# A decoder trunk on one core: the MLP's second product interleaved with the first of the next quarter, five of eight K-pairs by seven products, and PSUM banks given by number

## The chip, the core and the metric

One core of a Trainium2 chip. TensorE (PE) multiplies, VectorE (DVE) and ScalarE (ACT) prepare operands and evacuate results, SyncE (SP) issues the loads of the weights. The metric is device microseconds for the whole kernel; a run counts the slowest core, here the only one.

## The reference

A trunk of two layers over one residual stream, 256 tokens by 2048 features, all in float32. Each layer has a mixer and a squared-ReLU MLP, both behind an RMS norm:

```
x = x + mix(rms_norm(x, norm_mix[layer]))
x = x + squared_relu_mlp(rms_norm(x, norm_mlp[layer]), mlp_w1[layer], mlp_w2[layer])

def squared_relu_mlp(h, w1, w2):
    return jnp.square(jax.nn.relu(h @ w1)) @ w2      # 2048 -> 8192 -> 2048
```

The change touches the MLP alone, and the way PSUM banks are named in the whole kernel.

## The kernel before

Every operand is float32 and is split into a hi part (rounded to the matmul's format) and a lo part (the remainder). A product is then three matmuls: hi by hi, hi by lo, lo by hi (`mm_three`, L145). For weights, ScalarE makes hi (`wh`, L129) and VectorE subtracts to get lo (`wl`, L130). Tiles of weights come by DMA into four buffers (`raw`), and hi and lo have four buffers each.

The MLP (`mlp`, L996) goes through the 8192 hidden features in four quarters of 2048. A quarter has two stretches.

*First product.* Eight chunks of 256 hidden features. A chunk is four steps (`steps_feats`, L252), each with 16 matmuls of 512 columns (hi weights) and 16 of 256 columns (lo weights) for four K-tiles. Both feature blocks of a chunk accumulate in a PSUM bank of their own. `evac_h` then adds the two halves of the bank (`both`: `bt_h` on ScalarE, `hu` on VectorE), applies relu and square, and splits the result into hi and lo. For the first four pairs of K-tiles (`SEVEN = 4`) it builds eight combinations of the four 128x128 blocks of the pair (`hp`, `pt`); for the other pairs it keeps them as they are (`ht`).

*Second product.* Two halves, of two 512-column blocks of the output each (`steps_seven`, L188). In a half there are eight pairs of K-tiles. A pair with combinations is a *seven step* (L199): Strassen's scheme, seven block products of three matmuls, 21 matmuls of 512 columns. Its weights need sums first: `ta` (L214), `tb` (L216, L217), and hi and lo of them. The products go to four banks of `pmis` (`ym`) and to three of the four of `pacc` (`yc`). The other pairs are *ordinary*: two steps (`eight`) with 12 matmuls each, 24 in all. The order of steps is written in the code: seven, two ordinary, seven, two ordinary, seven, seven, and the rest. After the last seven step the four `ym` banks are combined and added to the residual (`early_y`), and after the last ordinary step the four `yc` banks (`late_y`).

In layer 1 the second half of the last quarter is the tail `finish`, without seven steps. In layer 0 the last half turns the new residual for the next layer (`nt_mix`) ahead of and behind its last step.

The program is a list of tiles and instructions; a scheduler puts each engine's instructions in an order of its own, and each engine then works its queue from front to end.

Of the kernel before, what the change touches and what calls it, by code (L numbers as in the profile page):

```python
# [9 lines left out]
F32 = mybir.dt.float32  # L10
# [4 lines left out]
P = 128  # L15
# [3 lines left out]
KD = D // P  # L19
FF = 8192  # L20
NQ = 4
SEVEN = 4
EPS = 1e-6
BIG = -3.0e38
MLA_SCALE = 192 ** -0.5
# [44 lines left out]
def trunk(ctx: ExitStack, tc: tile.TileContext, plan, a, c_first, c_even, c_odd, out):  # L70
# [3 lines left out]
    xpool = ctx.enter_context(tc.tile_pool(name="xpool", bufs=1))  # L74
    tpool = ctx.enter_context(tc.tile_pool(name="tpool", bufs=1))
    wpool = ctx.enter_context(tc.tile_pool(name="wpool", bufs=1))
    pacc = ctx.enter_context(tc.tile_pool(name="pacc", bufs=4, space=bass.MemoryType.PSUM))
    pmis = ctx.enter_context(tc.tile_pool(name="pmis", bufs=4, space=bass.MemoryType.PSUM))

    n_t = [0]  # L80
# [9 lines left out]
        n_t[0] += 1  # L90
        return mpool[0].tile([P, 2, S], FR, name=f"M{n_t[0]}", tag="M", bufs=17)

    def acc(name):
        return pacc.tile([P, 512], F32, name=name, tag="acc")

    def mis(name):
        return pmis.tile([P, 512], F32, name=name, tag="mis")
# [88 lines left out]

    def steps_seven(pool, H, pairs, w, c, early, late, name="y"):

        box = {}
        rest = [k for k in range(len(H) // 2) if k not in pairs]

        def seven(k):  # L200
            def go():
                first, last = k == pairs[0], k == pairs[-1]
                if first:
                    box["m"] = {i: mis(f"{name}m{i}") for i in (1, 5, 7, 6)}
                    box["c"] = {i: acc(f"{name}c{i}") for i in ((0, 1), (1, 0), (0, 0), (1, 1))}
                m, cc = box["m"], box["c"]
                pt = H[2 * k][0]
                r0 = load(w, [(2 * k, c, 512), (2 * k + 1, c + 512, 512)], (2, 512))
                r1 = load(w, [(2 * k, c + 512, 512), (2 * k + 1, c, 512)], (2, 512))
                n_w[0] += 1  # L210
                ta = pool.tile([P, 2, 512], F32, name=f"ta{n_w[0]}", tag="ta", bufs=2)
                tb = pool.tile([P, 2, 512], F32, name=f"tb{n_w[0]}", tag="tb", bufs=1)
                h0, l0 = halves(r0)
                nc.vector.tensor_tensor(ta, r0, r1[:, 0:1, :].to_broadcast([P, 2, 512]), OP.add)  # L214
                h1, l1 = halves(ta, pool, "t", 3)
                nc.vector.tensor_tensor(tb[:, 0, :], ta[:, 0, :], r0[:, 1, :], OP.add)  # L216
                nc.vector.tensor_tensor(tb[:, 1, :], tb[:, 0, :], r1[:, 1, :], OP.add)  # L217
                h2, l2 = halves(tb, pool, "t", 3)
                h3, l3 = halves(r1[:, 1:2, :])

                def product(ac, i, h, l, j, last):
                    mm_three(ac, (pt[:, 0, i, :], pt[:, 1, i, :]), (h[:, j, :], l[:, j, :]), first, last)

                end = last and not rest
                product(m[1], 1, h0, l0, 0, last)
                product(m[5], 5, h1, l1, 0, last)
                product(m[7], 4, h1, l1, 1, last)
                product(m[6], 6, h2, l2, 0, last)
                product(cc[1, 0], 3, h2, l2, 1, end)
                product(cc[0, 1], 7, h0, l0, 1, end)  # L230
                product(cc[0, 0], 0, h3, l3, 0, end)
                if last:
                    early(m[1], m[5], m[6], m[7])
            return go

        def eight(k, j):
            def go():
                cc = box["c"]
                hi, lo = weights(w, 2 * k, 2, c + 512 * j, 512)
# [8 lines left out]
        out, rest_of = [], iter(rest)  # L248
        for i, k in enumerate(pairs):
            out.append([seven(k)])  # L250
            if i != len(pairs) - 2:
                out += [[eight(r, j) for j in range(2)] for r in [next(rest_of)]]  # L252
        out += [[eight(r, j) for j in range(2)] for r in rest_of]
        return sum(out, [])

    def steps_feats(Ts, w, c0, evac, n=256, name="f"):

        box = {}
        groups = [range(i, i + 4) for i in range(0, len(Ts), 4)]

        def make(gi, g):
            def go():
                if gi == 0:
                    box["a"] = [acc(f"{name}{f}") for f in range(n // P)]
                hi, lo = weights(w, g[0], 4, c0, n)
# [157 lines left out]
    def weave(main, side):  # L423

        done = 0
        for i, go in enumerate(main):
            go()
            want = (i + 1) * len(side) // max(1, len(main))
            while done < want:
                side[done]()  # L430
                done += 1
        for go in side[done:]:
            go()

    class Late:
# [561 lines left out]
    def mlp(layer, norm, nxt):  # L997
# [6 lines left out]
        def evac_h(H):  # L1004
            def make(c):
                box = {}

                def go(f, ac):
                    u = sm.tile([P, S], F32, name="hu", tag="hu", bufs=2)
                    both(sm, u, ac, "h")  # L1010
                    nc.scalar.activation(u, u, AF.Relu)  # L1011
                    if c >= SEVEN:
                        r = sm.tile([P, S], F32, name="hr", tag="hr", bufs=2)
                        nc.scalar.activation(r, u, AF.Square)
                        H[2 * c + f] = sm.tile([P, 2, S], FR, name="ht", tag="ht", bufs=2 * (NF // 2 - SEVEN) + 1)
                        split_to(H[2 * c + f], r)
# [36 lines left out]

        def late_y(c):
            def go(cc):
                for b, j in ((1, 0), (0, 1), (0, 0), (1, 1)):
# [4 lines left out]
        def evac_y(c):  # L1061
# [2 lines left out]
                    nc.vector.scalar_tensor_tensor(x[b][c], ac[b], scale["s"][:, b:b + 1], x[b][c], OP.mult, OP.add)  # L1064
            return go

        for q in range(NQ):
            H = [None] * NF
            ev = evac_h(H)
            for c in range(NF // 2):  # L1070
                steps = steps_feats(X, ("mlp_w1", layer, 0), q * (FF // NQ) + c * 256, ev(c), name="h")
                if q == 0 and c == 0:
                    run(steps[:3])
                    norm.turn(3)
                    run(steps[3:])
                    norm.close()
                    scale["s"] = norm.inv_var()
                else:
                    run(steps)
            wq = ("mlp_w2", layer, q * (FF // NQ))  # L1080
            last = q == NQ - 1
            for c in (0, 2):
                if last and nxt is None and c == 2:
                    finish(H, wq, evac_y, scale, sm)
                    break
                steps = steps_seven(sm, H, list(range(SEVEN)), wq, c * 512, early_y(c), late_y(c))
                if last and c == 2:
                    nxt.stats(0)
                    nxt.stats(1)
                    steps = steps[:-1] + [lambda: nxt.turn(0)] + steps[-1:] + [lambda: nxt.turn(1)]  # L1090
                run(steps)
        if nxt is not None:
            nxt.stats(2)
            nxt.stats(3)
# [64 lines left out]
```

## Time and profile before

| | us |
|---|---|
| median of 3 runs | 2175.98 (2175.11 to 2176.67) |
| the profiled execution | 2174.26 |
| its span, first to last instruction | 2172.5 |
| TensorE busy | 2131.6 |
| VectorE busy | 1607.7 |
| ScalarE busy | 1216.2 |

Part 1 of the page gives the busy time of each engine as an average over the whole span; the stages differ, so the timeline and the windows have to be read stage by stage. Matmuls overlap in the records (one of 512 columns lasts about 0.39 us and the next starts about 0.23 us after it), so how fast TensorE goes is read from start to start. A row of the busy time by stage reads: stretch, its length, then busy us (instructions) of PE, PEld, DVE, ACT and POOL, the granted TensorE clock (1.00 is 2.4 GHz), the share of DMA and GB/s. In brackets behind a row of the timeline stands how long the engine was idle before it and what ended that.

### The profile page before, as it was taken

Reading aid. Unit: us, or ns where it says so; the run is one execution under the profiler, and the core shown is the slowest. Engines: PE = TensorE matmul, PEld = TensorE weight load, DVE = VectorE, ACT = ScalarE, POOL = GpSimd, SP = SyncE. Lnnn points to the kernel's source line nnn. Section 1 sums busy time; section 2 is a strip of 40 time slices with the busy share of each in tenths; the row PEclk is TensorE's granted clock in tenths of the full one; section 3 lists DMA queues with packets and bytes.
Section 4 is the critical chain, followed back from the end, with each engine's and each line's share of the span. In section 5 each row is a group of like instructions: output and inputs, shape, how many; then the busy total and the mean of one; then the engine's idle time right before and its main releaser. Section 6 shows DMA issues by size and latency. Waiting matters only on the chain.

```text
span 2172.5 us, 29631 instructions
## 1 busy us (share of the span) xinstructions
PE 2131.6 (98%) x11034; PEld 1826.3 (84%) x11034; DVE 1607.7 (74%) x2265; ACT 1216.2 (56%) x1833; POOL 5.6 (0%) x12
## 2 busy tenths in 40 slices
PE   9999999999999999999999999999999999999998
PEld 8988888887887887887888888888878878878887
DVE  5678556698679679768977667556896797698685
ACT  6676445654664565565644444556655655655664
POOL 0000000000000000000000000000000000000000
PEclk9999999999999999999999999999999999999999
DMA  8554455556555655655555555455555556556654
GB/s 293 168 175 162 158 180 184 186 173 208 190 184 186 202 179 180 207 182 181 187 193 174 176 173 175 165 185 184 184 192 196 184 176 212 185 178 208 206 186 153
DMA packets 115281, 404.53 MB, mean 186 GB/s; under 512 B 12929, under 2 KB 13569, under 8 KB 115137
## 3 DMA queue, kind: packets, MB, share of 16 engines
q1 hardware_dynamic: 114624, 401.07, 56.3%
q8 instruction: 87, 1.43, 0.3%
q0 software_dynamic: 368, 1.51, 0.2%
q14 instruction: 58, 0.47, 0.1%
q10 hardware_dynamic: 144, 0.06, 0.0%
HBM read 400.49 MB, written 2.10 MB: 185 GB/s over the span
## 4 chain that ended last, share of the span: by engine, by line
PE 78%; DVE 14%; DMA 4%; issue 3%; ACT 1%; SPq 0%; DVEq 0%; POOLq 0%; POOL 0%; ACTq 0%
PE h L158 19%; PE h L162 10%; DVE wl L130 7%; DMA wr<-in_mlp_w 4%; PE q L158 3%; PE k L158 3%; PE o L150 3%; PE o L148 3%; PE o L149 3%; PE v L148 2%; PE v L150 2%; PE v L149 2%; DVE ta L214 2%; PE k L162 1%; PE q L162 1%
## 5 line engine op out<-in xcount | busy, mean ns | idle before, releaser
L130 DVE TENSOR_TENSOR wl<-wr,wh 128x1024 fp32r<-128x1024 f32 (+4 forms) x769 | 884.2, 1155 | 429.1 <-ACT wh L129 422.2
L129 ACT ACTIVATE wh<-wr 128x1024 fp32r<-128x1024 f32 (+4 forms) x769 | 768.2, 1003 | 676.2 <-PE h L158 197.9
L158 PE MATMUL h<-T,wh 128*128 128x512 f32 x2048 | 513.4, 392 | 0.0
L158 PEld LDWEIGHTS h<-T,wh 128*128 128x128 f32 x2048 | 368.4, 189 | 66.9 <-DVE T L296 1.1
L162 PEld LDWEIGHTS h<-T,wl 128*128 128x128 f32 x2048 | 279.4, 190 | 20.0
L162 PE MATMUL h<-T,wl 128*128 128x256 f32 x2048 | 285.6, 282 | 0.0
L148 PE MATMUL ym<-wh,pt 128*128 128x512 f32 x240 | 95.2, 401 | 16.0 <-ACT wh L129 15.9
L149 PE MATMUL ym<-wl,pt 128*128 128x512 f32 x240 | 97.5, 406 | 10.8 <-DVE wl L130 10.7
L129 ACT ACTIVATE wh<-ta 128x1024 fp32r<-128x1024 f32 x60 | 63.6, 1061 | 77.3 <-DVE ta L214 77.2
L148 PE MATMUL o<-wh,M 128*128 128x512 f32 x256 | 102.3, 399 | 0.0
L214 DVE TENSOR_TENSOR ta<-wr,wr 128x1024 f32<-128x1024 f32 x60 | 73.3, 1221 | 37.1 <-DMA wr<-in_mlp_w 36.8
L129 ACT ACTIVATE wh<-tb 128x1024 fp32r<-128x1024 f32 x60 | 63.2, 1053 | 66.6 <-DVE tb L217 66.6
L150 PE MATMUL o<-wh,M 128*128 128x512 f32 x256 | 99.8, 390 | 0.0
L149 PE MATMUL o<-wl,M 128*128 128x512 f32 x256 | 99.7, 389 | 0.0
L150 PE MATMUL ym<-wh,pt 128*128 128x512 f32 x240 | 94.8, 395 | 0.0
L130 DVE TENSOR_TENSOR wl<-tb,wh 128x1024 fp32r<-128x1024 f32 x60 | 73.3, 1221 | 22.9 <-ACT wh L129 22.9
L1011 ACT ACTIVATE hu<-hu 128x256 f32<-128x256 f32 x128 | 50.5, 408 | 51.3 <-DVE hu L278 51.3
L148 PE MATMUL v<-wh,T 128*128 128x512 f32 x192 | 77.4, 403 | 0.0
L130 DVE TENSOR_TENSOR wl<-ta,wh 128x1024 fp32r<-128x1024 f32 x60 | 73.1, 1219 | 2.7 <-ACT wh L129 2.7
L150 PE MATMUL v<-wh,T 128*128 128x512 f32 x192 | 74.9, 390 | 0.0
L149 PE MATMUL v<-wl,T 128*128 128x512 f32 x192 | 74.8, 390 | 0.0
L148 PEld LDWEIGHTS ym<-wh,pt 128*128 128x128 f32 x240 | 44.9, 189 | 30.0 <-ACT wh L129 21.7
(991 smaller groups left out, 3644.2 us busy)
## 6 DMA issues: line engine op xcount, KB each, us to landing
wr<-in_mlp_w SPq DMA_DIRECT2D x512, 512.0 KB, 3.6
wr<-in_od_w_qkv SPq DMA_DIRECT2D x96, 512.0 KB, 4.1
wr<-in_ev_w_in SPq DMA_DIRECT2D x32, 512.0 KB, 3.5
wr<-in_ev_w_out SPq DMA_DIRECT2D x32, 512.0 KB, 3.4
wr<-in_od_w_out SPq DMA_DIRECT2D x32, 512.0 KB, 3.5
wr<-in_ev_w_in SPq DMA_DIRECT2D x24, 344.0 KB, 3.0
wr<-in_ev_w_in SPq DMA_DIRECT2D x15, 364.0 KB, 5.8
wr<-in_mla_w_ukv SPq DMA_DIRECT2D x8, 512.0 KB, 3.5
```

What stands on the lines that cost most here:

```text
L129: nc.scalar.activation(hi, raw, AF.Copy)
L130: nc.vector.tensor_tensor(lo, raw, hi.bitcast(F32), OP.subtract)
L148: nc.tensor.matmul(ac, xh, hi, start=first, stop=False)
L149: nc.tensor.matmul(ac, xh, lo, start=False, stop=False)
L150: nc.tensor.matmul(ac, xl, hi, start=False, stop=last)
L158: nc.tensor.matmul(acs[f], hi[:, j, f * P:(f + 1) * P], Ts[j].rearrange("p a t -> p (a t)"), start=first and j == 0, stop=False)
L162: nc.tensor.matmul(acs[f][:, :S], lo[:, j, f * P:(f + 1) * P], Ts[j][:, 0, :], start=False, stop=last and j == n - 1)
L214: nc.vector.tensor_tensor(ta, r0, r1[:, 0:1, :].to_broadcast([P, 2, 512]), OP.add)
L1011: nc.scalar.activation(u, u, AF.Relu)
```

## The change

Three things are changed, with the arithmetic of the reference kept.

1. `SEVEN` is 5: in a half five pairs are seven steps and three are ordinary. The last half of layer 0 has three and five.
2. A seven step is cut into two parts: `go_a` (loads, sums, splits, and products 1, 5 and 7 into `ym`; 9 matmuls) and `go_b` (products 6, 3, 2 and 4; 12 matmuls). The first product is cut into 16 blocks of 128 features, two steps of eight K-tiles each. `woven` runs blocks and parts of seven steps in turn: in the first half of a quarter the last eight blocks of that quarter, in the second half the first eight blocks of the next. The ordinary steps of a half follow together. The first half of the first quarter of a layer is still made in chunks of 256.
3. `acc` gives each of the four banks a tag of its own. Chunks elsewhere take the banks in turn; in the woven part products 3, 2 and 4 have banks 0, 1 and 2, and all blocks of the first product have bank 3, which goes to the fourth `yc` when the ordinary steps begin.

`hr` is no longer a tile of its own, the square is written in place; the late adds come in another order.

```diff
-SEVEN = 4
+SEVEN = 5
...
-    def acc(name):
-        return pacc.tile([P, 512], F32, name=name, tag="acc")
+    def acc(name, bank=None):
+
+        if bank is None:
+            bank = n_a[0] % 4
+            n_a[0] += 1
+        return pacc.tile([P, 512], F32, name=name, tag=f"acc{bank}", bufs=1)
...
+            def go_a():
                 if first:
                     box["m"] = {i: mis(f"{name}m{i}") for i in (1, 5, 7, 6)}
...
                 product(m[1], 1, h0, l0, 0, last)
                 product(m[5], 5, h1, l1, 0, last)
                 product(m[7], 4, h1, l1, 1, last)
+
+            def go_b():
+                if first:
+                    box["c"] = {i: acc(f"{name}c{i[0]}{i[1]}", n) for n, i in enumerate(((1, 0), (0, 1), (0, 0)))}
+                m, cc = box["m"], box["c"]
+                product(m[6], 6, *t[2], 0, last)
+                product(cc[1, 0], 3, *t[2], 1, end)
+                product(cc[0, 1], 7, *t[0], 1, end)
+                product(cc[0, 0], 0, *t[3], 0, end)
                 if last:
                     early(m[1], m[5], m[6], m[7])
...
+    def woven(main, side):
+
+        done = 0
+        for i, go in enumerate(main):
+            want = -(-(i + 1) * len(side) // len(main))
+            run(side[done:want])
+            done = want
             go()
...
+            def block(i):
+                def go():
+                    run(steps_feats(X, ("mlp_w1", layer, 0), q * (FF // NQ) + i * P,
+                                    lambda f, ac: ev[i // 2](i % 2, ac), n=P, name="h", kt=8, bank=3))
+                return go
...
         for q in range(NQ):
+            last = q == NQ - 1
+            wq = ("mlp_w2", layer, q * (FF // NQ))
+            seven, eight = steps_seven(sm, H, list(range(SEVEN)), wq, 0, early_y(0), late_y(0))
+            woven(hs[NF // 2:], sum(seven, []))
+            run(*eight)
+            if last and nxt is None:
+                finish(H, wq, evac_y, scale, sm)
+                break
+            pairs = list(range(3 if last else SEVEN))
+            seven, eight = steps_seven(sm, H, pairs, wq, 1024, early_y(2), late_y(2))
...
+            hs, _ = blocks(q + 1, H)
+            sv = sum(seven, [])
+            woven(hs[:NF // 2], sv)
+            run(*eight)
```

What this does to the queues is seen in the built programs' order. TensorE of before, layer 0, where the first product of the second quarter (`h`) ends and the second product begins (`ym` is a product of a seven step, `wl` and `wh` the halves of its weights):

```order
L162 MATMUL h_5919<-T_3623,wl_5989 128x256
L162 MATMUL h_5919<-T_3631,wl_5989 128x256
L162 MATMUL h_5919<-T_3634,wl_5989 128x256
L148 MATMUL ym_6028<-wh_6042,pt 128x512
L149 MATMUL ym_6028<-wl_6043,pt 128x512
L150 MATMUL ym_6028<-wh_6042,pt 128x512
L148 MATMUL ym_6029<-wh_6047,pt 128x512
```

TensorE of the change, layer 0, in the second half of the first quarter: the end of the third seven step's first products, and the fourth block `h` of the second quarter:

```order
L156 MATMUL ym_4806<-wh_5075,pt 128x512
L154 MATMUL ym_4807<-wh_5081,pt 128x512
L155 MATMUL ym_4807<-wl_5082,pt 128x512
L156 MATMUL ym_4807<-wh_5081,pt 128x512
L154 MATMUL yc_4842<-wh_5081,pt 128x512
L164 MATMUL h_5098<-T_3252,wh_5101 128x512
L164 MATMUL h_5098<-T_3255,wh_5101 128x512
```

One matmul of product 3 (`yc`) stands ahead of the block; its other two, and products 2 and 4, stand behind the block's 32 matmuls.

VectorE of before, layer 0, where the second half of the second quarter begins (`x` from `yc` is a late add; `ta` and `tb` are the sums of the first seven step; `wl` from `wr` is lo of plain weights):

```order
L130 TENSOR_TENSOR wl_6394<-wr_6387,wh_6393 128x1024
L1058 SCALAR_TENSOR_TENSOR x_73<-yc(0, 0)_6034,iv_mlp_3681,x_73 128x512
L1058 SCALAR_TENSOR_TENSOR x_77<-yc(1, 0)_6033,iv_mlp_3681,x_77 128x512
L214 TENSOR_TENSOR ta_6391<-wr_6387,wr_6389 128x1024
L130 TENSOR_TENSOR wl_6409<-wr_6389,wh_6408 128x512
L1058 SCALAR_TENSOR_TENSOR x_74<-yc(0, 1)_6032,iv_mlp_3681,x_74 128x512
L1058 SCALAR_TENSOR_TENSOR x_78<-yc(1, 1)_6035,iv_mlp_3681,x_78 128x512
L130 TENSOR_TENSOR wl_6399<-ta_6391,wh_6398 128x1024
L216 TENSOR_TENSOR tb_6392<-ta_6391,wr_6387 128x512
L130 TENSOR_TENSOR wl_6436<-wr_6433,wh_6435 128x1024
```

VectorE of the change, layer 0, second half of the first quarter: the queue between the evacuations (`hu`) of the second and the third block of the next quarter:

```order
L136 TENSOR_TENSOR wl_5076<-ta_5068,wh_5075 128x1024
L228 TENSOR_TENSOR tb_5069<-tb_5069,wr_5066 128x512
L136 TENSOR_TENSOR wl_5071<-wr_5064,wh_5070 128x1024
L1041 TENSOR_TENSOR hp<-hp 128x256
L136 TENSOR_TENSOR wl_5086<-wr_5066,wh_5085 128x512
L1042 TENSOR_TENSOR hp<-hp 128x128
L136 TENSOR_TENSOR wl_5082<-tb_5069,wh_5081 128x1024
L1043 TENSOR_TENSOR hp<-hp 128x128
L136 TENSOR_TENSOR wl_5102<-wr_5099,wh_5101 128x1024
L1046 TENSOR_TENSOR pt<-hp,pt 128x1024
L136 TENSOR_TENSOR wl_5124<-wr_5121,wh_5123 128x1024
L286 TENSOR_TENSOR hu<-h_5012,bt_h 128x256
```

Between two evacuations now stand the rest of the third seven step's weights, the combinations of a finished pair (`hp`, `pt`) and the weights of the next block (`wl_5102`, `wl_5124`); the last row frees bank 3.

## Rows read from the trace of the kernel before

**Rows 1.** The page, part 1: busy us (share) xinstructions.
```profile
PE 2131.6 (98%) x11034; PEld 1826.3 (84%) x11034; DVE 1607.7 (74%) x2265; ACT 1216.2 (56%) x1833; POOL 5.6 (0%) x12
```

**Rows 2.** Busy time by stage: the eight second-product stretches (first, fourth, all together).
```profile
445.41:533.68 88.27, 84.61 (x362) 68.35 (x361) 80.93 (x93) 46.29 (x56) 0.00 (x0) 0.98 0.56 185
...
978.46:1069.97 91.51, 87.09 (x371) 70.02 (x370) 82.31 (x95) 51.07 (x71) 0.00 (x0) 0.96 0.55 182
...
sum 662.00, PE 635.26 PEld 513.76 DVE 605.35 ACT 353.70 POOL 0.00; mean PE 79.41 PEld 64.22 DVE 75.67 ACT 44.21 POOL 0.00
```

**Rows 3.** Busy time by stage: one first-product stretch, the second quarter.
```profile
533.68:623.04 89.36, 89.36 (x513) 78.66 (x512) 60.08 (x76) 54.62 (x87) 0.00 (x0) 1.00 0.59 194
```

**Rows 4.** Waits of TensorE: us in total, times, longest us.
```profile
PE ym L148 <- ACT wh L129: 15.9, 8, 2.2
PE ym L149 <- DVE wl L130: 10.7, 12, 1.2
```

**Rows 5.** Timeline of TensorE (start, us, engine, line): two matmuls one seven step apart.
```profile
625.79 0.39 PE L148 MATMUL yc(1, 0)_6033<-wh,pt 128*128 128x512 f32 x1
...
635.99 0.39 PE L148 MATMUL yc(1, 0)_6033<-wh,pt 128*128 128x512 f32 x1
```

**Rows 6.** Timeline of VectorE where the second half of the second quarter begins.
```profile
661.34 0.74 DVE L1058 SCALAR_TENSOR_TENSOR x<-yc(0, 0)_6034,iv_mlp,x 128x512 f32<-128x512 f32 x1
662.00 0.73 DVE L1058 SCALAR_TENSOR_TENSOR x<-yc(1, 0)_6033,iv_mlp,x 128x512 f32<-128x512 f32 x1
...
665.71 1.21 DVE L130 TENSOR_TENSOR wl<-ta,wh 128x1024 fp32r<-128x1024 f32 x1
```

**Rows 7.** Timeline of TensorE at the same place, with waits in brackets.
```profile
666.98 0.50 PE L149 MATMUL ym<-wl,pt 128*128 128x512 f32 x1 [1.22 <-DVE wl L130]
...
670.40 0.50 PE L148 MATMUL ym<-wh,pt 128*128 128x512 f32 x1 [2.23 <-ACT wh L129]
...
671.49 0.63 PE L150 MATMUL yc(0, 1)_6383<-wh,pt 128*128 128x512 f32 x1
671.91 0.63 PE L148 MATMUL yc(0, 0)_6385<-wh,pt 128*128 128x512 f32 x1
...
674.47 0.54 PE L150 MATMUL yc(0, 0)_6385<-wh,pt 128*128 128x512 f32 x1
```

**Rows 8.** Timeline of TensorE in the third quarter, behind a short wait.
```profile
828.68 0.50 PE L149 MATMUL ym<-wl,pt 128*128 128x512 f32 x1 [0.54 <-DVE wl L130]
829.01 0.40 PE L150 MATMUL ym<-wh,pt 128*128 128x512 f32 x1
829.25 0.39 PE L148 MATMUL yc(1, 0)_7611<-wh,pt 128*128 128x512 f32 x1
```

**Rows 9.** Timeline of VectorE: four kinds of instruction, back to back.
```profile
615.50 1.22 DVE L130 TENSOR_TENSOR wl<-wr,wh 128x1024 fp32r<-128x1024 f32 x1
616.63 0.75 DVE L293 TENSOR_TENSOR ht<-hr,ht 128x256 fp32r<-128x256 f32 x2
617.30 0.68 DVE L216 TENSOR_TENSOR tb<-ta,wr 128x512 f32<-128x512 f32 x1
617.90 0.68 DVE L130 TENSOR_TENSOR wl<-wr,wh 128x512 fp32r<-128x512 f32 x1
```

**Rows 10.** Timeline of TensorE in the first product.
```profile
561.59 2.00 PE L158 MATMUL h<-T,wh 128*128 128x512 f32 x8
...
564.38 2.00 PE L158 MATMUL h<-T,wh 128*128 128x512 f32 x8
```

**Rows 11.** Groups by line: x, busy us, mean ns, idle before.
```profile
L278 DVE TENSOR_TENSOR hu<-h,bt_h 128x256 f32<-128x256 f32 x128 | 47.9, 416 | 0.0
...
L277 ACT ACTIVATE bt_h<-h 128x256 f32<-128x256 f32 x128 | 40.9, 370 | 0.0
...
L1026 DVE TENSOR_TENSOR hp<-hp 128x128 f32<-128x128 f32 x32 | 9.4, 293 | 1.1
```

**Rows 12.** DMA issues: x, KB each, median us to landing.
```profile
wr<-in_mlp_w SPq DMA_DIRECT2D x512, 512.0 KB, 3.6
```

More of the change, by code (lines that the diff above doesn't have):

```diff
@@ L76, in trunk @@
     wpool = ctx.enter_context(tc.tile_pool(name="wpool", bufs=1))
-    pacc = ctx.enter_context(tc.tile_pool(name="pacc", bufs=4, space=bass.MemoryType.PSUM))
+    pacc = ctx.enter_context(tc.tile_pool(name="pacc", bufs=1, space=bass.MemoryType.PSUM))
     pmis = ctx.enter_context(tc.tile_pool(name="pmis", bufs=4, space=bass.MemoryType.PSUM))
@@ L91, in m_tile @@
         return mpool[0].tile([P, 2, S], FR, name=f"M{n_t[0]}", tag="M", bufs=17)
[L93 to L94 removed]
+    n_a = [0]
+    def acc(name, bank=None):
[3 more added lines that the diff above has]
+        return pacc.tile([P, 512], F32, name=name, tag=f"acc{bank}", bufs=1)
     def mis(name):
@@ L200, in seven, with product @@
         def seven(k):
-            def go():
-                first, last = k == pairs[0], k == pairs[-1]
+            first, last = k == pairs[0], k == pairs[-1]
+            end = last and not rest
+            t = {}
+            def product(ac, i, h, l, j, last):
+                pt = H[2 * k][0]
+                mm_three(ac, (pt[:, 0, i, :], pt[:, 1, i, :]), (h[:, j, :], l[:, j, :]), first, last)
+            def go_a():
                 if first:
                     box["m"] = {i: mis(f"{name}m{i}") for i in (1, 5, 7, 6)}
-                    box["c"] = {i: acc(f"{name}c{i}") for i in ((0, 1), (1, 0), (0, 0), (1, 1))}
-                m, cc = box["m"], box["c"]
-                pt = H[2 * k][0]
+                m = box["m"]
                 r0 = load(w, [(2 * k, c, 512), (2 * k + 1, c + 512, 512)], (2, 512))
@@ L212, in go @@
                 tb = pool.tile([P, 2, 512], F32, name=f"tb{n_w[0]}", tag="tb", bufs=1)
-                h0, l0 = halves(r0)
+                t[0] = h0, l0 = halves(r0)
                 nc.vector.tensor_tensor(ta, r0, r1[:, 0:1, :].to_broadcast([P, 2, 512]), OP.add)
@@ L217, in go @@
                 nc.vector.tensor_tensor(tb[:, 1, :], tb[:, 0, :], r1[:, 1, :], OP.add)
[L218 to L224, printed above, removed]
+                t[2] = halves(tb, pool, "t", 3)
+                t[3] = halves(r1[:, 1:2, :])
                 product(m[1], 1, h0, l0, 0, last)
@@ L227, in go @@
                 product(m[7], 4, h1, l1, 1, last)
[L228 to L231, printed above, removed]
+            def go_b():
[6 more added lines that the diff above has]
+                product(cc[0, 0], 0, *t[3], 0, end)
                 if last:
                     early(m[1], m[5], m[6], m[7])
-            return go
+            return [go_a, go_b]
         def eight(k, j):
@@ L238, in go @@
                 cc = box["c"]
+                if k == rest[0] and j == 1:
+                    cc[1, 1] = acc(f"{name}c11", 3)
                 hi, lo = weights(w, 2 * k, 2, c + 512 * j, 512)
@@ L246, in eight, with steps_feats @@
             return go
[L248 to L256, printed above, removed]
+        return [seven(k) for k in pairs], [[eight(k, j) for j in range(2)] for k in rest]
+    def steps_feats(Ts, w, c0, evac, n=256, name="f", kt=4, bank=None):
         box = {}
-        groups = [range(i, i + 4) for i in range(0, len(Ts), 4)]
+        groups = [range(i, i + kt) for i in range(0, len(Ts), kt)]
         def make(gi, g):
@@ L263, in go @@
                 if gi == 0:
-                    box["a"] = [acc(f"{name}{f}") for f in range(n // P)]
-                hi, lo = weights(w, g[0], 4, c0, n)
+                    box["a"] = [acc(f"{name}{f}", bank) for f in range(n // P)]
+                hi, lo = weights(w, g[0], kt, c0, n)
                 mm_feats(box["a"], [Ts[k] for k in g], hi, lo, gi == 0, gi == len(groups) - 1)
@@ L432, in weave @@
         for go in side[done:]:
+            go()
+    def woven(main, side):
[4 more added lines that the diff above has]
+            done = want
             go()
@@ L1012, in go @@
                     if c >= SEVEN:
[L1013 to L1016, printed above, removed]
+                        nc.scalar.activation(u, u, AF.Square)
+                        H[2 * c + f] = sm.tile([P, 2, S], FR, name="ht", tag="ht", bufs=2 * (NF // 2 - SEVEN))
+                        split_to(H[2 * c + f], u)
                         return
@@ L1055, in go @@
             def go(cc):
-                for b, j in ((1, 0), (0, 1), (0, 0), (1, 1)):
+                for b, j in ((1, 1), (1, 0), (0, 1), (0, 0)):
                     v = x[b][c + j]
@@ L1065, in evac_y, with blocks @@
             return go
-        for q in range(NQ):
-            H = [None] * NF
[L1069 to L1091, printed above, removed]
+        def blocks(q, H):
+            ev = evac_h(H)
+            def block(i):
[3 more added lines that the diff above has]
+                return go
+            ev = [ev(c) for c in range(NF // 2)]
+            return [block(i) for i in range(NF)], ev
@@ new lines, in mlp @@
+        H = [None] * NF
+        hs, ev = blocks(0, H)
+        steps = steps_feats(X, ("mlp_w1", layer, 0), 0, ev[0], name="h")
+        run(steps[:3])
+        norm.turn(3)
+        run(steps[3:])
+        norm.close()
+        scale["s"] = norm.inv_var()
+        for c in range(1, NF // 4):
+            run(steps_feats(X, ("mlp_w1", layer, 0), c * 256, ev[c], name="h"))
+        for q in range(NQ):
+            last = q == NQ - 1
[8 more added lines that the diff above has]
+            seven, eight = steps_seven(sm, H, pairs, wq, 1024, early_y(2), late_y(2))
+            if last:
+                nxt.stats(0)
+                nxt.stats(1)
+                steps = sum([a + b for a, b in zip(seven, eight)] + eight[len(seven):], [])
+                run(steps[:-1], [lambda: nxt.turn(0)], steps[-1:], [lambda: nxt.turn(1)])
+                break
+            H = [None] * NF
+            hs, _ = blocks(q + 1, H)
+            sv = sum(seven, [])
+            woven(hs[:NF // 2], sv)
+            run(*eight)
```

## The prediction

> **What bounds the kernel now.** I read the page's busy times first, then busy time by stage, then who TensorE waits for, then the rows of those waits. TensorE is busy for 98% of the span [rows 1]: whatever moves the time must take matmuls away or close the few holes between them. By stage the picture splits. In a first-product stretch TensorE has no hole (89.36 us busy of 89.36), and VectorE works 60 us of it [rows 3]. In a second-product stretch (two halves, 360 matmuls) VectorE works 81 us of 88 and TensorE is not full [rows 2]. All of TensorE's listed waits there are for the halves of weights that ScalarE and VectorE make, 15.9 and 10.7 us in total [rows 4].
>
> What would a full TensorE need? From one seven step to the next, 21 + 24 = 45 matmuls of 512 columns, 10.20 us pass: 0.227 us each [rows 5]. The eight stretches last 662.0 us together (the sum in [rows 2]). They hold 7 x 360 + 180 = 2700 matmuls, 612.0 us, and eight transposes of 0.1 us. The excess is 662.0 - 612.0 - 0.8 = 49.2 us: the 26.6 us of waits, and the start-up and the lower clock behind them.
>
> Where it arises is seen at the start of a second half. VectorE has no idle time in brackets there: the late adds of the half before stand between the weights of the new seven step, `wl<-ta` starts at 665.71 and takes 1.21 us [rows 6]. TensorE waits 1.22 us for it until 666.98, then 2.23 us for ScalarE's `wh<-tb`; behind that matmuls start 0.42 us apart (671.49, 671.91) instead of 0.23, until 674.47 [rows 7]. That is 1.2 GHz, the lower of the two levels of the clock, for 8 matmuls: 1.6 us. The mean granted clock of such a stretch is 0.98, in the fourth 0.96 [rows 2], against 1.00 in the first product [rows 3].
>
> **The change, part by part.**
>
> *Fewer matmuls.* Seven products are 21 matmuls, an ordinary pair 24. Layer 0 goes from 8 x 4 = 32 seven steps to 7 x 5 + 3 = 38, layer 1 from 7 x 4 = 28 to 7 x 5 = 35: 13 more, 39 matmuls fewer, 39 x 0.227 = 8.8 us, all on TensorE, which sets the end.
>
> *More VectorE work.* Back to back an instruction takes 1.13 us at 1024 columns, 0.60 at 512, 0.33 at 256 (two in 0.67) [rows 9], an add to the residual 0.66 [rows 6]. A seven step is `ta`, three wide `wl`, one narrow `wl` and two `tb`: 4 x 1.13 + 3 x 0.60 = 6.3 us; an ordinary pair is 2 x 1.13 = 2.3. So 13 x 4.0 = 52 us more on VectorE, which was 74% busy [rows 1]. Beside matmuls that costs nothing; without that cover up to all 52 us.
>
> *The interleaving gives the cover.* Before, a half is 4 seven steps, 4 ordinary pairs, the early combination (4 adds to the residual, 4 of 0.60: 5.0 us) and the late adds (2.6): VectorE 25.2 + 9.1 + 7.6 = 41.9 us against 180 x 0.227 = 40.8 us of TensorE. VectorE is the longer one, while the first product beside it has 29 us of VectorE to spare. Now a half holds 8 blocks of the first product too. A block is 32 matmuls, twice the 2.79 us from 561.59 to 564.38 [rows 10], 5.59 us. TensorE: 8 x 5.59 + 177 x 0.227 = 84.9 us. VectorE: 5 x 6.3 + 6 x 1.13 (ordinary) + 16 x 1.13 (weights of the blocks) + 7.6 + 8 x 0.33 (`hu`) + 4 x 2.1 (`hp`, `pt`) = 75 us where four pairs are prepared, 71 where one is. So VectorE is 12% under TensorE instead of over it. In the woven part alone it is close, 68 us each; VectorE brings a lead from the six ordinary steps (16.3 us of matmuls, 6.8 of VectorE). If this holds, the 49.2 us go. What is late next is the next term.
>
> *A wait is added.* All blocks of a half accumulate in bank 3, so a block's first matmul waits for the `hu` add of the block before. On VectorE this add stands behind weights already queued; on TensorE everything stands behind the block. I followed one half by hand through the queues with these durations. Between two blocks TensorE has 9 matmuls (2.0 us), 12 (2.7) or 13 (2.9), and the evacuation itself is `bt_h` 0.37 and `hu` 0.42 us [rows 11]. The tightest place is the fourth block, whose VectorE queue is the last one shown with the change. From the end of the second block VectorE has one `wl` and its `hu`, 1.6 us, then the twelve rows: 6 wide x 1.13 + 2 x 0.60 + 0.33 + 2 x 0.29 [rows 11] + 0.42 = 9.3 us; 10.9 in all. TensorE has 12 matmuls, a block, 9 and 4 matmuls: 25 x 0.227 + 5.59 = 11.3 us. Margin 0.4 us. The second block comes out at 0.1 to 0.2 us (9 matmuls against a `wl`, `hu` and two hand-overs), the others between 0.3 and 1.9. Before, chunks changed banks, so the trace has no price of this wait. Bounds: nothing, if the margins hold; one more wide VectorE instruction, 1.13 us, at each of 14 halves x 7 waits, 111 us. I take 0.5 us a half, by the margins: 7 us.
>
> *Loads.* Their number stays; one of 512 KB lands 3.6 us after its issue [rows 12]. By hand the loads of a seven step are issued 4 to 7 us ahead of `ta`; the tightest margin, 0.5 us, is inside the 7 us. If the landing were 1 us longer, up to 1 us a half, 14 us.
>
> *The rest.* The late adds' new order and the square in place change no instruction's kind: nothing. In the mixers the scheduler swaps some rows, whose worth no row shows: I put 3 us either way on it, a sixteenth of the excess found here.
>
> **Sum.** Against the profiled execution, 2174.3 us: - 8.8 - 49.2 + 7 = 2123. The median of the runs shown is 1.7 us above that execution: 2125 us.
>
> **Rivals.**
>
> *VectorE still sets the pace.* In the woven part its 68 us equal TensorE's, and at 92% busy it lost time before. If each of 14 halves keeps what a half lost, 49.2 / 15 = 3.3 us, 46 us come back: 2116 + 46 + 2 = 2164. For it: margins of tenths. Against: VectorE enters each woven part with a lead.
>
> *Bank 3 stops TensorE*: slower than before. If `hu` comes late at each block by one wide subtraction and the evacuation, 1.13 + 0.42 + 0.37 = 1.9 us, TensorE idles 98 x 1.9 = 186 us: 2116 + 186 + 2 = 2304. It decides from 58 / 98 = 0.6 us a block. For it: one bank, and adds queued behind weights whose buffers the same matmuls free. Against: by hand that instruction fits in at every block, if barely.
>
> On the clock the rows show a fall behind waits of 1.22 and 2.23 us [rows 7]; behind one of 0.54 us matmuls go on 0.24 us apart [rows 8]. The Trainium skill (TensorE: Matmul & The Clock Gate, section "A second HAM failure mode: psum-queue depth-cycling") tells of a kernel whose groups of matmuls, cycling through PSUM banks, left TensorE idle briefly but often, so that the clock swung and throughput was lost. By that rule each of the 98 bank waits could cost a fall's 1.6 us, 157 us in all, and the time would be 2275. [Rows 8] speaks against it; it shares the chance of the rival above.
>
> *Nothing comes of it*: new waits eat both terms, 58 us, 4.1 us a half: 2176.
>
> **Chances.** Forecast (2112 to 2136) 0.72; VectorE sets the pace (up to 2170) 0.16; nothing 0.04; bank 3 or the clock 0.08. A measurement here tells a change of 0.2%, 4.4 us, from none. So faster 0.88, within 0.04, slower 0.08. The range goes from no new wait and 6 us of luck in mixers and loads (2116 + 2 - 6 = 2112) to the first rival, 2164; the loads' 14 us lie inside.
>
> **What would show it.** Right: TensorE's listed waits on `ym` all but gone, no matmuls 0.42 us apart in the second product, a granted clock of 0.99 and more there, VectorE's busy time up by some 50 us, a block `h` waiting well under 1 us. Wrong: `h` waiting for `hu` at every block, which is bank 3; waits for `wl` and `wh` as long as before, which is the first rival; or a span that shrinks by more than 58 us, which none of these explains.

## The result, and the profile after

The changed kernel takes 2152.87 us (median of four runs, 2148.98 to 2153.71) beside 2176.32 for the kernel before: a ratio of 0.989 (95% interval 0.987 to 0.991). The forecast was 2125. The direction and the range hold; of the 51 us forecast, 23 came.

First the page of the changed kernel, part 1 [rows 1 were the kernel before]. Its span is 2147.1 us, its profiled execution took 2148.98, the fastest of the four.

```profile
PE 2116.2 (99%) x10995; PEld 1808.9 (84%) x10995; DVE 1667.3 (78%) x2346; ACT 1249.1 (58%) x1851; POOL 5.6 (0%) x12
```

There are 39 matmuls fewer, as counted, and VectorE is busy for 60 us more (52 were forecast). Next, the busy time by stage of the kernel before (layer 0's MLP, the odd mixer, layer 1's MLP), and then of the changed kernel. Columns as in [rows 2].

```profile
354.88:1070.76 715.88, 700.25 (x3516) 591.27 (x3514) 567.54 (x685) 413.03 (x596) 0.00 (x1) 0.99 0.57 188
1070.76:1455.30 384.54, 384.54 (x2014) 329.70 (x2012) 258.76 (x469) 188.65 (x302) 1.44 (x2) 1.00 0.55 177
1455.30:2119.46 664.16, 653.05 (x3320) 554.12 (x3318) 522.88 (x634) 385.89 (x559) 1.10 (x2) 0.99 0.59 191
```
```profile
356.03:1054.86 698.83, 690.72 (x3497) 581.60 (x3496) 595.88 (x724) 429.24 (x604) 0.00 (x1) 1.00 0.59 193
1054.86:1440.08 385.22, 384.78 (x2014) 329.95 (x2012) 258.33 (x468) 188.44 (x302) 1.44 (x2) 1.00 0.54 176
1440.08:2094.12 654.04, 646.96 (x3298) 545.79 (x3297) 555.27 (x678) 402.92 (x569) 1.11 (x2) 1.00 0.59 195
```

The two MLPs shrink by 17.1 and 10.1 us; the first starts 1.1 us later and the odd mixer takes 0.7 us more. The forecast took 8.8 and 49.2 us out of the MLPs and put 7 back. What came out is 27.2, so 58.0 - 27.2 = 30.8 us of new cost stand where 7 were put.

TensorE's longest waits of the changed kernel show where (columns as in [rows 4]).

```profile
PE h L164 <- DVE hu L286: 14.3, 34, 1.0
PE c L154 <- ACT wh L135: 4.3, 1, 4.3
```

Both waits of [rows 4] on `ym` are gone; the one for `c` lies outside the MLP. In their place `h` waits for `hu`: a block of the first product for the add that frees bank 3. A second profile of the unchanged file (below) gives 18.0 us in 45 such waits, in a span 4.1 us longer.

Here are two blocks of the changed kernel on TensorE, the first with such a wait in front and the second without.

```profile
543.90 0.40 PE L154 MATMUL ym<-wh,pt 128*128 128x512 f32 x1
...
545.74 0.39 PE L156 MATMUL ym<-wh,pt 128*128 128x512 f32 x1
546.55 2.11 PE L164 MATMUL h<-T,wh 128*128 128x512 f32 x8 [0.43 <-DVE hu L286]
...
552.25 0.40 PE L154 MATMUL ym<-wh,pt 128*128 128x512 f32 x1
...
554.77 0.39 PE L156 MATMUL yc<-wh,pt 128*128 128x512 f32 x1
555.00 1.98 PE L164 MATMUL h<-T,wh 128*128 128x512 f32 x8
...
560.56 0.40 PE L154 MATMUL yc<-wh,ht 128*128 128x512 f32 x1
```

Read from start to start. Without a wait the block starts 0.23 us after the last matmul ahead of it (554.77 to 555.00) and takes 5.56 us. With one it starts 0.81 us after it (545.74 to 546.55) and takes 5.70. The price is 0.58 + 0.14 = 0.72 us, where the bracket lists 0.43: 0.29 us more. Added up in this way over all 112 woven blocks of the trace, the 34 listed waits cost 24.5 us, 0.72 each, and 17 blocks that start late after an idle time too short for the list cost 5.7. With 0.3 us at a few others that is 30.4 of the 30.8 us: nearly all of the new cost stands at the start of these blocks. In the second profile it is 34.2 us. (A block is 32 matmuls, 16 of 512 and 16 of 256 columns. A chunk of the kernel before is two blocks, so each of its four steps has 8 and 8 matmuls, not the 16 and 16 of its description; [rows 3] have 513 for eight chunks.)

VectorE and then ScalarE of the changed kernel show why `hu` is late there. The block before had its last matmul just ahead of 543.90.

```profile
542.60 1.22 DVE L136 TENSOR_TENSOR wl<-wr,wh 128x1024 fp32r<-128x1024 f32 x1
543.80 1.23 DVE L136 TENSOR_TENSOR wl<-tb,wh 128x1024 fp32r<-128x1024 f32 x1
544.95 1.22 DVE L136 TENSOR_TENSOR wl<-wr,wh 128x1024 fp32r<-128x1024 f32 x1
546.08 0.42 DVE L286 TENSOR_TENSOR hu<-h,bt_h 128x256 f32<-128x256 f32 x1
```
```profile
542.71 1.06 ACT L135 ACTIVATE wh<-tb 128x1024 fp32r<-128x1024 f32 x1 [1.30 <-DVE tb L228]
543.68 1.04 ACT L135 ACTIVATE wh<-wr 128x1024 fp32r<-128x1024 f32 x1
544.63 0.36 ACT L285 ACTIVATE bt_h<-h 128x256 f32<-128x256 f32 x1
```

Two wide subtractions stand between the block's end and `hu`, 2.3 us, and TensorE has 2.04 us of other matmuls. From 542.71 on neither engine idles ahead of its part of the evacuation; both are working off weights. Of the 34 listed waits 21 stand behind 9 matmuls like this one, 6 behind 12 and 7 behind 13. The second place, in layer 0's first woven half, shows TensorE, VectorE and ScalarE in turn.

```profile
419.98 0.40 PE L154 MATMUL ym<-wh,pt 128*128 128x512 f32 x1
...
422.50 0.39 PE L156 MATMUL yc<-wh,pt 128*128 128x512 f32 x1
423.80 0.96 PE L164 MATMUL h<-T,wh 128*128 128x512 f32 x3 [0.91 <-DVE hu L286]
```
```profile
420.32 1.23 DVE L225 TENSOR_TENSOR ta<-wr,wr 128x1024 f32<-128x1024 f32 x1 [1.57 <-DMA wr<-in_mlp_w]
421.58 0.69 DVE L227 TENSOR_TENSOR tb<-ta,wr 128x512 f32<-128x512 f32 x1
422.19 1.22 DVE L136 TENSOR_TENSOR wl<-wr,wh 128x1024 fp32r<-128x1024 f32 x1
423.33 0.42 DVE L286 TENSOR_TENSOR hu<-h,bt_h 128x256 f32<-128x256 f32 x1
```
```profile
421.58 1.06 ACT L135 ACTIVATE wh<-ta 128x1024 fp32r<-128x1024 f32 x1 [1.29 <-DVE ta L225]
422.55 0.36 ACT L285 ACTIVATE bt_h<-h 128x256 f32<-128x256 f32 x1
```

The block is done at 419.98. On VectorE `ta` waits for a load until 420.32, and `ta`, a `tb` and a `wl` stand ahead of `hu`. On ScalarE `wh<-ta` stands ahead of `bt_h`, but `bt_h` is done at 422.91, 0.42 us before `hu` starts, so VectorE's own queue decides. It is so elsewhere too: in the whole kernel `hu` waits for `bt_h` for 1.3 us in 8. Five of the 34 listed waits are of this second kind, with VectorE waiting for a load between the block's end and `hu`; they are 3.6 of the 14.3 us. At the other 29 VectorE works from the block's end to `hu` without a listed pause, as at the first place.

### The profile page after: what moved, and what is told of

It reads as the page before. It is cut to its first block, busy times and chain, and to the rows that moved or that the text cites. A ratio compares the mean times of both kernels' runs of the same rounds, so it can differ in the third digit from the quotient of the medians.

```text
span 2147.1 us, 29491 instructions
## 1 busy us (share of the span) xinstructions
PE 2116.2 (99%) x10995; PEld 1808.9 (84%) x10995; DVE 1667.3 (78%) x2346; ACT 1249.1 (58%) x1851; POOL 5.6 (0%) x12
## 5 line engine op out<-in xcount | busy, mean ns | idle before, releaser
L164 PE MATMUL h<-T,wh 128*128 128x512 f32 x2048 | 518.1, 395 | 15.2 <-DVE hu L286 14.3
L154 PE MATMUL yc<-wh,ht 128*128 128x512 f32 x360 | 140.3, 390 | 0.0
L155 PE MATMUL yc<-wl,ht 128*128 128x512 f32 x360 | 140.2, 389 | 0.0
L156 PE MATMUL yc<-wh,ht 128*128 128x512 f32 x360 | 140.1, 389 | 0.0
L155 PE MATMUL ym<-wl,pt 128*128 128x512 f32 x292 | 114.5, 392 | 0.0
L154 PE MATMUL ym<-wh,pt 128*128 128x512 f32 x292 | 114.5, 392 | 0.0
L156 PE MATMUL ym<-wh,pt 128*128 128x512 f32 x292 | 113.6, 389 | 0.0
L225 DVE TENSOR_TENSOR ta<-wr,wr 128x1024 f32<-128x1024 f32 x73 | 89.2, 1222 | 30.6 <-DMA wr<-in_mlp_w 30.3
L135 ACT ACTIVATE wh<-tb 128x1024 fp32r<-128x1024 f32 x73 | 76.9, 1053 | 35.5 <-DVE tb L228 35.2
L135 ACT ACTIVATE wh<-ta 128x1024 fp32r<-128x1024 f32 x73 | 77.0, 1055 | 30.4 <-DVE ta L225 30.2
L155 PE MATMUL yc<-wl,pt 128*128 128x512 f32 x235 | 91.8, 390 | 0.0
L154 PE MATMUL yc<-wh,pt 128*128 128x512 f32 x235 | 91.7, 390 | 0.0
L156 PE MATMUL yc<-wh,pt 128*128 128x512 f32 x235 | 91.6, 390 | 0.0
```

The lines of the kernel that those rows point to most:

```text
L135: nc.scalar.activation(hi, raw, AF.Copy)
L154: nc.tensor.matmul(ac, xh, hi, start=first, stop=False)
L155: nc.tensor.matmul(ac, xh, lo, start=False, stop=False)
L156: nc.tensor.matmul(ac, xl, hi, start=False, stop=last)
L164: nc.tensor.matmul(acs[f], hi[:, j, f * P:(f + 1) * P], Ts[j].rearrange("p a t -> p (a t)"), start=first and j == 0, stop=False)
```

## The experiments

Three theories. *Theory 1, the bank:* `hu` in its queue keeps bank 3 shut. *Theory 2, VectorE's pace:* the woven part has too much VectorE work, and the bank is only where it shows. *Theory 3, the loads:* `ta` waits for a load 36 times in the changed kernel, 30.3 us, and `hu` stands behind. (In the kernel before, `ta` waited 31 times, 36.8 us.)

**The changed kernel again**, beside three of the kernels below.

> The changed kernel again, unaltered, beside the three below on one chip: 2148 to 2154 us, and waits of h for hu between 13 and 16 us. If these waits differ by more than 2 us from the first profile, differences of that size between the other kernels count for nothing.

Measured: 2153.15 us (2149.56 to 2153.49), ratio 0.990 (0.988 to 0.991). The waits came out at 18.0 us, more than expected, so differences of some 4 us between two profiles say nothing.

**ScalarE frees the bank.**

```diff
-                    both(sm, u, ac, "h")
+                    t = sm.tile([P, 2 * S], F32, name="hb", tag="hb", bufs=2)
+                    nc.scalar.activation(t, ac, AF.Copy)
+                    nc.vector.tensor_add(u, t[:, :S], t[:, S:])
```

> The changed kernel with one edit: ScalarE copies a block's whole accumulator (512 columns) out of bank 3, and VectorE's hu adds from that copy, so VectorE no longer frees the bank. The changed kernel's first and second products hold 31.5 us more than their matmuls need, and TensorE's waits of h for hu are 14.3 us in 34. Theory 1 (the bank): those waits go, and with them most of the 31.5 us; h waits for ScalarE's copy for under 5 us in all, the time is 2122 to 2132 us. Theory 2 (VectorE sets the pace of the woven part, the bank is only where it shows): the waits move to m and c products waiting for wl and wh, 10 us and more in all, and the time stays within 2145 to 2155 us.

Measured: 2127.44 us (2125.83 to 2131.24), ratio 0.978 (0.977 to 0.979), 25 us under the changed kernel. TensorE's longest wait in the MLPs, the page, and two halves by stage:

```profile
PE h L164 <- ACT hb L1028: 4.2, 7, 1.2
```
```profile
PE 2107.3 (99%) x10995; PEld 1810.7 (85%) x10995; DVE 1663.3 (78%) x2346; ACT 1275.7 (60%) x1851; POOL 5.6 (0%) x12
```
```profile
498.95:584.61 85.66, 85.59 (x436) 72.31 (x434) 76.56 (x95) 54.90 (x72) 0.00 (x0) 1.00 0.61 196
584.61:670.08 85.47, 85.19 (x435) 72.38 (x434) 73.47 (x90) 54.16 (x75) 0.00 (x0) 1.00 0.61 200
```

The same two halves of the changed kernel:

```profile
500.72:587.22 86.50, 85.70 (x435) 72.31 (x434) 76.80 (x94) 53.46 (x72) 0.00 (x0) 1.00 0.59 195
587.22:675.28 88.06, 86.34 (x436) 72.13 (x435) 72.78 (x88) 52.66 (x75) 0.00 (x0) 1.00 0.58 191
```

VectorE does as much as in the changed kernel (1663 us against 1667) and as many instructions, yet a half falls to 85.5 us, near the 84.9 that the forecast worked out, and late starts of blocks, added up as above, fall from 30.4 to 9.6 us (the two profiled spans lie 17.7 us apart). Theory 1 holds; theory 2 does not. One copy on an engine with room is worth 25 of the 28 us that the forecast lacked. Part of this may be another order: an edit lets the scheduler order the queues anew, and here 434 of VectorE's 2346 places hold another instruction than in the changed kernel.

**A finer weave.** A step in seven parts of one product, so that 12 to 15 matmuls stand between blocks.

```diff
-            return [go_a, go_b]
+            return [go_a,
+                    lambda: product(box["m"][5], 5, *t[1], 0, last),
+                    lambda: product(box["m"][7], 4, *t[1], 1, last),
+                    lambda: product(box["m"][6], 6, *t[2], 0, last),
+                    go_c,
+                    lambda: product(box["c"][0, 1], 7, *t[0], 1, end),
+                    go_z]
```

> The changed kernel with one edit: a seven step is woven in seven parts of one product each, so that 12 to 15 matmuls stand between two blocks in place of 9, 12 and 21. No instruction is added. Theory 1 (the bank): the waits after 9 matmuls (2.04 us) shrink; h waits for hu are at most half of the 14.3 us, the time 2130 to 2142 us. Theory 2 (VectorE sets the pace): the same work on VectorE in the same time, waits of the same sum elsewhere; 2145 to 2155 us.

Measured: 2141.40 us (2137.35 to 2142.26), ratio 0.984 (0.983 to 0.985).

```profile
PE ym L155 <- DVE wl L136: 8.1, 12, 1.2
...
PE h L164 <- DVE hu L291: 3.1, 4, 1.2
```

The bank's waits fall from 14.3 to 3.1 us, as theory 1 has it, but `ym` waits for `wl` come back, 8.1 us. With the bank nearly out of the way, the weights that VectorE makes are next.

**Both edits together.**

> Both edits together: ScalarE's copy frees the bank, and seven parts of a step are spread over the blocks. Theory 1 (the bank): no wait at the bank is left, 2118 to 2128 us. Theory 2 (VectorE sets the pace): waits for wl and wh as long as the ones at the bank before, 2145 to 2155 us.

Measured: 2141.75 us (2138.34 to 2147.37), ratio 0.985 (0.984 to 0.987). No wait at the bank is listed, but `ym` waits for `wl` for 9.1 us in 11. Theory 1's number missed by 14 us: with the finer weave the copy gains nothing. Why `wl` is late there is left open.

**Four pairs by seven products, interleaved.** `SEVEN = 4` in the changed kernel, nothing else.

> The changed kernel with four pairs by seven products in place of five: 59 seven steps for 73, so 42 matmuls more (9.5 us) and some 56 us less on VectorE. The interleaving and the fixed banks stay. A half then has a part of 9 and a part of 12 matmuls by turns between its blocks. Theory 1 (the bank): as many places with 9 matmuls between blocks as before or more, so waits of h for hu stay above 10 us, excess 22 to 35 us, time 2149 to 2162 us. Theory 2 (VectorE sets the pace): with 10% less of VectorE's work in a woven half the waits fall under 4 us, excess under 10 us, time 2130 to 2137 us.

Measured: 2155.97 us (2155.19 to 2156.53), ratio 0.991 (0.990 to 0.992).

```profile
PE h L164 <- DVE hu L286: 10.7, 15, 1.7
PE h L164 <- DVE x L1074: 5.3, 9, 1.0
```

VectorE is busy for 1599.6 us, 68 less than in the changed kernel, and `h` still waits 16 us for bank 3, now also for the late add of the half before, which reads the same bank. Theory 2 fails. Taking off the 9.5 us for 42 matmuls, the lighter VectorE saves 6 us. Beside the kernel before (2174.9 us in this comparison), which also has four pairs, the interleaving with its blocks and fixed banks is worth 19 us.

**Five pairs, nothing interleaved.** The kernel before with `SEVEN = 5`; the ordinary steps are placed so that the last one comes after the last seven step.

```diff
-SEVEN = 4
+SEVEN = 5
...
-            if i != len(pairs) - 2:
+            if i != len(pairs) - 2 and i < len(rest) - 1:
...
-                steps = steps_seven(sm, H, list(range(SEVEN)), wq, c * 512, early_y(c), late_y(c))
+                steps = steps_seven(sm, H, list(range(3 if last and c == 2 else SEVEN)), wq, c * 512, early_y(c), late_y(c))
```

> The kernel before with five pairs of a half by seven products (three in the last half of layer 0) and nothing interleaved; banks as before. 39 matmuls fewer, 13 seven steps more. If VectorE is the longer engine of a half that is not interleaved, as the forecast had it (41.9 us before, 45.9 us now, against 40 us of TensorE), a half grows from 44 to about 48 us and the time is 2205 to 2235 us. If VectorE is not what limits such a half, only the matmuls count: 2163 to 2176 us.

Measured: 2191.68 us (2190.80 to 2192.07), ratio 1.007 (1.006 to 1.009): slower than before.

```profile
PE ym L149 <- DVE wl L130: 31.8, 16, 3.8
PE ym L148 <- ACT wh L129: 7.2, 7, 1.7
```

Neither range holds. The waits say that VectorE is the longer engine of such a half, but the loss is smaller than expected: 17 us more in all, or 26 counting the 8.8 us of matmuls saved, of the 52 us of added VectorE work. (The granted clock over the span is 0.987 here and 0.992 before, so the clock has a part in it.) So the extra seven steps lose time by themselves, and with five pairs the interleaving is worth 2191.7 - 2152.9 = 39 us. The fifth pair itself saves only 3 us in the interleaved kernel (2156.0 to 2152.9), of the 9.5 that its matmuls take.

**One more load buffer** in the changed kernel. The second load of a seven step gets a buffer of its own; to make room, `yp` and `yq` share the buffers of `hp`.

```diff
-                r1 = load(w, [(2 * k, c + 512, 512), (2 * k + 1, c, 512)], (2, 512))
+                r1 = load(w, [(2 * k, c + 512, 512), (2 * k + 1, c, 512)], (2, 512), pool, 1)
...
-                p = sm.tile([P, 512], F32, name="yp", tag="yp", bufs=1)
-                q = sm.tile([P, 512], F32, name="yq", tag="yq", bufs=1)
+                t = sm.tile([P, 8, P], F32, name="yp", tag="hp", bufs=2).rearrange("p a b -> p (a b)")
+                p, q = t[:, :512], t[:, 512:]
```

> The changed kernel with one load of each seven step in a buffer of its own (five in place of four; the combination's scratch shares the buffers of hp to make the room). VectorE's ta waits for its load 36 times, 30.3 us, and hu stands behind it in VectorE's queue. Theory 1 (the bank and VectorE's order alone): ta comes earlier but hu stands behind as many instructions; h still waits for hu 10 us and more, 2145 to 2154 us. Theory 3 (the late load is what makes hu late): ta's wait for the load falls under 10 us, h's for hu under 7 us, the time is 2130 to 2142 us.

Measured: 2140.05 us (2138.59 to 2141.64), ratio 0.984 (0.982 to 0.986).

```profile
PE h L164 <- DVE hu L286: 9.5, 19, 1.3
```

The time is theory 3's, 13 us under the changed kernel; the waits (9.5 us) lie between the two. But theory 3's own sign is wrong: `ta` waits for its load for 66.1 us now, not under 10. A possible reading, which no run shows, is that VectorE now comes to `ta` earlier and waits there for a load that is needed later. The listed wait of `ta` does not tell what loads cost: in the kernel where ScalarE frees the bank it is 70.7 us, and that one is 25 us faster.

**The control:** the changed kernel with only the shared scratch.

> The changed kernel with the combination's scratch (yp, yq) in the buffers of hp and no other edit: what the kernel with one more load buffer also had. If the load buffer brought that kernel's gain, this one is as the changed kernel, 2147 to 2154 us with 12 us and more of h's waits for hu. If sharing the scratch brought it, this one is at 2138 to 2144 us.

Measured: 2153.37 us (2150.15 to 2157.07), ratio 0.990 (0.988 to 0.991), `h` waiting 14.5 us in 34. The edit of the load buffer brought the gain, not the scratch. Whether earlier loads did it is not shown: beside this control, 456 of VectorE's 2346 places and 274 of ScalarE's 1851 hold another instruction in the kernel with the load buffer.

**The copy and the load buffer**, with the shared scratch.

> ScalarE's copy frees the bank, and one load of each seven step has a buffer of its own. With the copy alone 4.2 us of waits at the bank were left in 7, where ScalarE's copy stood behind weights of a ta that had waited for its load. Theory 1: that is the ScalarE's own order, 2124 to 2130 us as without the buffer. Theory 3 (late loads): those waits go, under 1.5 us is left, and the time is 2117 to 2123 us.

Measured: 2142.00 us (2136.88 to 2144.28), ratio 0.984 (0.982 to 0.987). Both theories missed: the bank waits 12.1 us in 9 for the copy. ScalarE's queue at one of the nine places:

```profile
515.65 1.06 ACT L1047 ACTIVATE pt<-hp 128x1024 fp32r<-128x1024 f32 x1 [1.10 <-DVE hp L1045]
516.61 1.04 ACT L135 ACTIVATE wh<-wr 128x1024 fp32r<-128x1024 f32 x1
517.56 0.58 ACT L1028 ACTIVATE hb<-h 128x512 f32<-128x512 f32 x1
```

The copy stands behind `pt`, and `pt` waits for VectorE, here and at seven of the other eight places. It is the same fault on the other engine. With the copy alone `pt` stood ahead of the copy at none of the seven places where the bank waited.

**The copy and the shared scratch**, without the load buffer.

> ScalarE's copy frees the bank, and the scratch shares the buffers of hp; four load buffers. With the fifth load buffer the bank waited 12.1 us for ScalarE's copy, against 4.2 us with the copy alone. If the fifth buffer's other order of ScalarE's queue did that, this one is as the copy alone, 2125 to 2131 us, 3 to 6 us of waits for the copy. If sharing the scratch did it, 2137 to 2144 us and over 9 us.

Measured: 2138.71 us (2137.14 to 2139.68), ratio 0.983 (0.982 to 0.985); waits for the copy 4.6 us in 11, and `ym` for `wh` 4.8 us in 6. Sharing two scratch tiles costs 11 us here and nothing in the control. It moves other instructions in both queues (354 of 2346 places on VectorE, 168 of 1851 on ScalarE); which of them costs it is left open.

**The copy and the load buffer without the shared scratch:** `hu` is added in place in `hb`, and `yq` takes a buffer of `hb`.

> ScalarE's copy frees the bank and one load of each seven step has a buffer of its own, this time without the shared scratch (hu is added in place in the copy, and yq takes its buffers). If the two cures are worth what each was alone, and only the shared scratch spoiled their sum, 2116 to 2124 us and under 2 us of waits for the copy. If ScalarE's own queue now sets when the bank comes free (the copy stands behind weights whose sums wait for a load, whatever the buffers), 2130 to 2145 us, with 6 us and more of waits for the copy.

Measured: 2138.64 us (2136.60 to 2139.49), ratio 0.983 (0.982 to 0.985), 12.5 us in 9 waits for the copy. The second answer holds in its numbers: ScalarE's own queue now sets when the bank comes free. Its reason does not: at all nine places the copy stands behind `pt`, which waits for `hp` on VectorE, and at none behind weights whose sums wait for a load.

**Six pairs**, with the copy and the shared scratch; `SEVEN = 6`.

> ScalarE's copy frees the bank, the scratch shares the buffers of hp, and six pairs of eight go by seven products: 42 matmuls fewer than with five (9.5 us) and 14 seven steps more, some 56 us more of VectorE. Theory 1 (the bank): the woven part has VectorE to spare, only the matmuls count, 2116 to 2124 us, or 2126 to 2134 us if sharing the scratch costs what it may. Theory 2 (VectorE sets the pace): waits of m products for wl of 15 us and more, 2136 to 2160 us.

Measured: 2136.28 us (2134.36 to 2140.64), ratio 0.983 (0.981 to 0.984), 2.4 us under the same kernel with five. Neither theory fits: the time is at the lower end of theory 2's range, but its waits for `wl` are not there, though VectorE is busy for 1726.2 us; `h` waits 8.1 us for `wh` and 6.0 for the copy, both ScalarE's, 14.1 us in all where with five pairs `ym` and `h` waited 9.4 for ScalarE. Of the 9.5 us that 42 fewer matmuls save, 2.4 come through.

## Why less than half of the forecast gain came

*Fewer matmuls, 8.8 us:* right, 39 fewer.

*The excess of 49.2 us goes:* right as far as it went. Both waits of [rows 4] are gone, the granted clock is 1.00 throughout both MLPs, and no half-speed matmuls as in [rows 7] are left. With five pairs and nothing interleaved these waits stay, 39.0 us in 23; with four pairs interleaved they are not listed. So the interleaving, with its blocks and banks, did it.

*VectorE 12% under TensorE in a half:* right within 2 us: it is 10% under. In the stretch from 500.72 VectorE is busy for 76.8 us (75 forecast) and TensorE's matmuls need the 84.9 us worked out: with the bank freed elsewhere a half takes 85.5.

*The mixers, 3 us either way:* 1.8 us more.

*A wait is added, 7 us:* this is the step that failed. The wait was seen, at the right place and with the right mechanism, and mis-sized: 30.8 us in place of 7, 2.2 us a half in place of 0.5. The hand count compared the sum of VectorE's work from one block's end to another with TensorE's, which gives margins of tenths of a microsecond, and it let VectorE enter with a lead. Here is the place that it called the tightest, the second to fourth block in the second half of layer 0's first quarter:

```profile
505.16 1.06 ACT L135 ACTIVATE wh<-wr 128x1024 fp32r<-128x1024 f32 x1 [1.30 <-PE h L164]
506.25 1.23 DVE L136 TENSOR_TENSOR wl<-wr,wh 128x1024 fp32r<-128x1024 f32 x1 [3.29 <-ACT wh L135]
507.75 1.23 DVE L225 TENSOR_TENSOR ta<-wr,wr 128x1024 f32<-128x1024 f32 x1 [0.27 <-DMA wr<-in_mlp_w]
508.70 0.40 PE L154 MATMUL ym<-wh,pt 128*128 128x512 f32 x1
...
511.08 1.22 DVE L136 TENSOR_TENSOR wl<-ta,wh 128x1024 fp32r<-128x1024 f32 x1
...
520.32 1.22 DVE L225 TENSOR_TENSOR ta<-wr,wr 128x1024 f32<-128x1024 f32 x1
520.45 2.11 PE L164 MATMUL h<-T,wh 128*128 128x512 f32 x8 [0.31 <-DVE hu L286]
```

The twelve rows from 511.08 to 520.32 take 9.2 us, as forecast (9.3). But from the second block's end at 508.70 to 511.08 VectorE needs 2.4 us, not 1.6: it is still at `ta` and has a `tb` and a `wl` ahead of `hu`. It came late because it had idled 3.29 us for a `wh`, which ScalarE could start only when a matmul of TensorE released it, and 0.27 us for a load. So VectorE was ahead, but could not use its lead. The margin of 0.4 us became a wait of 0.31. In 12 of the 34 listed waits VectorE idled like this for a `wh` or a load after the `hu` before; in the other 22, this one among them, it had no listed pause between the two `hu` and was working off what stood in its queue. The count took each instruction as ready when its turn came. It also priced a wait by its idle time, and each costs 0.29 us more.

*Loads, hidden, 14 us if later by 1 us:* the value taken for it was wrong too. The median landing of all loads is still 3.6 us, as in [rows 12], but the 36 loads that `ta` waits for landed 4.7 us after their issue (median; 4.8 for the one at 420.32), and the 31 of the kernel before 4.5. The forecast counted with the median of all. How much of the 30.8 us hangs on loads stays open: directly it is five listed waits, 3.6 us, and the 13 us of a fifth buffer may be another order of the queues. SyncE's queue waits for VectorE's `wl` to free a buffer for 1299.9 us in 536, but it did so for 1166.0 us in 521 in the kernel before.

*The rivals.* "VectorE still sets the pace" gave 2164, 11 us off where the forecast was 28 off, but not by its mechanism: 68 us less of VectorE's work saved 6 us, and a change of engine for the bank saved 25 with VectorE's work unchanged. It had in part the place, since at 22 of the 34 waits VectorE worked without a listed pause; that its number came nearer than the forecast is luck. "Bank 3 stops TensorE" had the mechanism and put the price at each of 98 blocks; listed are 34 to 45, of 0.4 us on average, which cost 0.7 each. With these waits, all at one bank, the granted clock is 1.00 without a break from 9.8 us to 2143 us. The rule named there (the Trainium skill, TensorE: Matmul & The Clock Gate, section "A second HAM failure mode: psum-queue depth-cycling"), by which frequent short stops of that kind make the clock swing, does not show here.

## What to carry to other kernels

When two streams share one accumulator bank, look for an engine whose queue has little ahead of the instruction that frees it, and list every instruction ahead of it in that queue with what *that* instruction waits for: what stands in the queue at that moment decides, not the sum of the work over a half. A margin of a few tenths of a microsecond, got by adding durations, is no margin when one instruction of the queue takes 1.1. The kernel in which ScalarE copies the bank is the best here, 2127.44 us, 2.2% under the kernel before and 1.2% under the changed one; its relatives with five pairs and other buffers take 2138.6 to 2142.0 us, so a small edit that lets the scheduler order the queues anew can cost 11 to 15 us of that gain.

## What was not expected of the hardware

A wait of TensorE for another engine costs more here than its bracket: 0.72 us start to start for a listed 0.43, and on average over the 34 waits 0.72 for 0.42. Of the extra 0.29 us, 0.14 lies in the block itself, whose first eight matmuls take 2.11 us in place of 1.98. It is not the clock, which is granted at 1.00 there.

A longer wait can go with a faster kernel. With the fifth buffer `ta`'s wait for its loads rose from 30.3 to 66.1 us, and the time fell by 13; with the copy on ScalarE it rose to 70.7, and the time fell by 25.
